# One end-of-block test with a whole-kernel repeat in place of four rechecks, and PSUM evacuations 300 places earlier in the order

## The chip, the cores and the metric

The kernel runs on one core of one Trainium2 chip. That core has five engines with queues of their own: TensorE (PE for matmuls, PEld for the load of the stationary operand), VectorE (DVE), ScalarE (ACT), GpSimd (POOL) and SyncE (SP), which issues nearly all DMAs. The metric is the device time of one execution in microseconds (us), lower is better.

## The reference

Two transformer blocks, one after the other, on one sequence of 1024 rows of width 1024, all in float32.

The first block has two layers. In each, the rows are normalised and modulated, projected, and go two ways: a spatial gating unit, and an attention in which every query row keeps only the 256 keys with the highest score of a small "indexer". That selection is what the change touches:

```python
logits = jnp.einsum('bthd,bsd->bths', qib, k_idx) * (IDX_DIM ** -0.5)
score = jnp.einsum('bth,bths->bts', wb, jax.nn.relu(logits)).astype(jnp.float32)
score = jnp.where(causal[None], score, -jnp.inf)
_, idx = lax.top_k(score, top)              # top = 256 of up to 1024 keys
...
p = jax.nn.softmax(sc, axis=-1).astype(v.dtype)
return jnp.einsum('bthk,btkd->bthd', p, v_sel)
```

The two ways are gated, concatenated, projected by `w_out`, added to the input and normalised. The second block (windowed attention, a short convolution, a router and 32 experts) follows; the change leaves its arithmetic alone.

## The kernel before

The program is written with a planner: Python code emits instructions in an order, each gets a priority from its place in that order, `tc.high_priority(offset=n)` places what it encloses n places further to the front, and the planner lays the instructions of every engine out on a simulated time line, taking the ready one with the best priority. On the chip each engine then runs its list strictly in that order.

A sequence is cut into 8 tiles of 128 rows, t or i = 0 to 7. Every float32 matmul is done with operands split in a high and a low part (`mm3`, L99 to L102: three matmuls); the split of a weight piece is an ACT copy (L108) and a POOL subtraction (L111).

One layer of the first block (`layer`) emits, in this order:

- for layer 2, the transposed input hT (`to_T`, L500: four PE transposes to one PSUM bank, then an ACT copy, L506, and a DVE subtraction, L507);
- projections (`dense_nat`), with `select` running beside them as two streams, tiles 2, 4, 6 and 3, 5, 7. `select(i)` transposes the indexer queries (`heads_T`, L535: PE L538, ACT L543, DVE L544), makes the scores (PE L628, ACT L631, DVE L634 and L636), scales them to 16-bit codes, stores the raw scores to DRAM (`scd`, L652), searches the threshold by counting (DVE L606 to L661), and takes the few remaining places by two MAX8. That handles at most 8 open places; a column of `fl` (L669) tells of a row with more. The result is a tile of 0 and -1e30, `bias[i]`, finished at L686;
- the gating unit `sgu`, a generator in the list `bgs` that is stepped beside the projections. It transposes its weights with `to_T` into `wmh` and `wml`, and its product leaves PSUM by one DVE instruction (L830);
- four pieces f = 0 to 3 of one more projection (`dense_T1`, PSUM banks `half`, evacuation L966 and L967), with the attention `attend` stepped beside them. It works in units of (tile, group, pair): `front` makes logits (PE L868), adds the bias and takes the row's extreme (DVE L869), exponentiates (ACT L872) and normalises (POOL L878); `back` transposes (PE L891), splits (ACT L899, DVE L900) and multiplies with the values (PE L904, L906); the pair of units ends with ACT L911 and DVE L912. Tiles 0 and 1 need only the causal bias; a tile from 2 on waits in `attend` until it is in `checked`;
- after piece f = 1 (`RA`) the emission of `select` is driven until tiles 4 and 5 are done, and then `recheck((2, 3, 4, 5))` is emitted; after 18 units (`RC`) `recheck((6, 7))`. A recheck adds the flags with a matmul (L752), reduces and compares them (DVE L754, L756), loads the answer into registers of DVE and SP (L757), takes three of the four buffers with the tag `w4` (the attention's `pt2` has the same tag), and opens a `tc.Switch` with two arms. Arm 1 loads the raw scores and computes the biases of these tiles exactly (`halves`, `choose`); arm 0 is empty. Since arm 1 writes `bias`, everything that reads `bias` of these tiles is behind the Switch;
- the load of `w_out` (L996, SP), split on ACT and POOL into the buffers `s32` that hT held, and the end of each tile: `fin1` (L1023, L1029, L1032) and `fin2` (48 matmuls on `half`, DVE L1045), with what is left of the attention.

At the very end of the program stands a loop `tc.For_i(0, nov, 1)` (L1735) over the experts' overflow blocks, whose count is loaded by every engine (L1730).

## Time and profile before

| | |
|---|---|
| time, median of 3 runs | 2373.92 us (2371.7 to 2374.93) |
| the profiled execution | 2371.94 us, span 2369.8 us |
| PE busy | 2140.5 us, 90% of the span |
| DVE busy | 1521.2 us, 64% |
| ACT and POOL busy | 1082.8 and 1082.0 us, 46% each |
| mean granted TensorE clock | 0.961 |

The span is the time from the first instruction to the last of that execution; the 2.1 us around it belong to the device time. Busy time counts an engine as working while an instruction runs; a matmul at the lower granted clock counts as busy for longer. Idle time in front of an instruction is put down to the semaphore that ended the wait. Layer 1 of the first block lies at about 45 to 690 us, layer 2 at 690 to 1320, the second block behind that.

### The profile page before, as it was taken

The numbers are of one execution on the slowest core, as the hardware profiler recorded it, in microseconds if no ns is written. First come the engines' busy times: TensorE is split into PE (matmuls) and PEld (weight loads), VectorE is DVE, ScalarE is ACT, GpSimd is POOL, SyncE is SP. The second block draws the span as 40 slices with busy tenths as digits, with TensorE's granted clock in tenths as the row PEclk, the third lists the DMA queues.
The fourth block names the chain that finished last, engine by engine and source line by source line (L and its number), as shares of the span: only waits on it lengthen the run. The fifth ranks groups of instructions, "written<-read, shape, count | busy, mean of one in ns | idle before, by whom it ended". The sixth has DMA issues, their size and how long they took to land. (4 is left out here: it accounts for less than half of the span.)

```text
span 2369.8 us, 35974 instructions
## 1 busy us (share of the span) xinstructions
PE 2140.5 (90%) x13235; PEld 1883.9 (79%) x13235; DVE 1521.2 (64%) x3191; ACT 1082.8 (46%) x1943; POOL 1082.0 (46%) x1018
## 2 busy tenths in 40 slices
PE   5998998798989979997998999999999797999896
PEld 4898897587879979876887888888888586888785
DVE  9768887677753769685776348861010345888784
ACT  4333443554642443436554335652121222778774
POOL 4664575556736553845554345532244412222221
PEclk9999998899999989998999999999999998999998
DMA  7522112312114111223111111122121256999994
GB/s 239 188 79 86 53 32 81 106 59 68 41 47 138 45 36 49 66 67 108 68 45 41 44 41 34 30 52 67 49 67 45 98 209 200 311 325 326 317 329 116
DMA packets 146392, 260.88 MB, mean 110 GB/s; under 512 B 24681, under 2 KB 101889, under 8 KB 133905
## 3 DMA queue, kind: packets, MB, share of 16 engines
q1 hardware_dynamic: 139024, 241.59, 31.1%
q0 software_dynamic: 7168, 16.79, 3.2%
q8 instruction: 105, 1.72, 0.3%
q14 instruction: 95, 0.77, 0.1%
HBM read 228.83 MB, written 37.90 MB: 113 GB/s over the span
## 5 line engine op out<-in xcount | busy, mean ns | idle before, releaser
L111 POOL TENSOR_TENSOR wlo<-wraw,whi 128x512 fp32r<-128x512 f32 (+1 forms) x188 | 249.8, 1329 | 484.9 <-ACT whi L108 459.2
L101 PE MATMUL big<-wlo,s 128*128 128x256 f32 (+1 forms) x1536 | 440.4, 288 | 16.0 <-POOL wlo L111 16.0
L100 PE MATMUL big<-whi,s 128*128 128x256 f32 (+1 forms) x1536 | 437.8, 289 | 13.6 <-ACT s L506 8.4
L102 PE MATMUL big<-whi,s 128*128 128x256 f32 (+1 forms) x1536 | 439.6, 288 | 0.0
L101 PEld LDWEIGHTS big<-wlo,s 128*128 128x128 f32 x1536 | 301.2, 196 | 22.8 <-POOL wlo L111 19.6
L100 PEld LDWEIGHTS big<-whi,s 128*128 128x128 f32 x1536 | 298.6, 196 | 21.9 <-ACT s L506 11.0
L102 PEld LDWEIGHTS big<-whi,s 128*128 128x128 f32 x1536 | 300.6, 196 | 3.1 <-issue 0.9
L108 ACT ACTIVATE whi<-wraw 128x512 fp32r<-128x512 f32 (+1 forms) x188 | 117.7, 627 | 385.2 <-PE big L102 127.2
L111 DVE TENSOR_TENSOR ew<-s,ew 128x1024 fp32r<-128x1024 f32 x138 | 162.8, 1220 | 39.0 <-ACT ew L108 37.9
L636 DVE SCALAR_TENSOR_TENSOR s<-rel,widx,s 128x384 f32<-128x384 f32 (+3 forms) x140 | 130.6, 957 | 85.1 <-ACT rel L631 83.6
L100 PE MATMUL sm<-ew,xT 128*96 128x256 f32 x512 | 147.6, 288 | 4.8 <-ACT xT L1636 4.8
L108 ACT ACTIVATE ew<-s 128x1024 fp32r<-128x1024 f32 x138 | 137.7, 1050 | 28.6 <-PE sm L102 18.8
L102 PE MATMUL sm<-ew,xT 128*96 128x256 f32 x512 | 148.6, 290 | 1.3 <-DVE xT L1637 1.2
L101 PE MATMUL sm<-ew,xT 128*96 128x256 f32 x512 | 146.3, 286 | 0.9 <-DVE ew L111 0.9
L631 ACT ACTIVATE rel<-sm 128x384 f32<-128x384 f32 (+3 forms) x160 | 80.5, 522 | 124.1 <-PE sm L628 114.7
L100 PE MATMUL half<-s,whi 128*128 128x512 f32 x320 | 130.7, 408 | 7.1 <-ACT s L953 3.1
L101 PE MATMUL half<-s,whi 128*128 128x512 f32 x320 | 128.7, 402 | 0.0
L102 PE MATMUL half<-s,wlo 128*128 128x512 f32 x320 | 127.3, 401 | 0.0
L1674 POOL DMA_INDIRECT out_dram<-yt,ti x32 | 58.2, 1820 | 136.0 <-DMA out_dram<-yt,ti 61.0
L606 DVE TENSOR_SCALAR_CACHE_REDUCE bias<-code,cand 128x512 bf16<-128x512 int16 (+5 forms) x126 | 114.1, 924 | 0.5
L878 POOL TENSOR_SCALAR Z<-Z,rc 128x128 f32<-128x128 f32 (+7 forms) x88 | 63.9, 738 | 83.3 <-DVE rc L876 50.7
L100 PE MATMUL big<-s,whi 128*128 128x512 f32 x256 | 99.7, 390 | 0.3 <-DVE convf L1335 0.3
(618 smaller groups left out, 6014.3 us busy)
## 6 DMA issues: line engine op xcount, KB each, us to landing
wraw<-in_w_in_dram SPq DMA_DIRECT2D x164, 256.0 KB, 2.8
adaw<-in_w_ada_dram SPq DMA_DIRECT2D x48, 512.0 KB, 4.5
s<-in_w_gate_e_dram SPq DMA_DIRECT2D x23, 1024.0 KB, 9.2
s<-in_w_up_e_dram SPq DMA_DIRECT2D x23, 1024.0 KB, 11.0
s<-in_w_down_e_dram SPq DMA_DIRECT2D x23, 1024.0 KB, 11.3
X<-in_w_gate_e_dram SPq DMA_DIRECT2D x9, 1024.0 KB, 10.1
X<-in_w_up_e_dram SPq DMA_DIRECT2D x9, 1024.0 KB, 9.8
X<-in_w_down_e_dram SPq DMA_DIRECT2D x9, 1024.0 KB
```

The source lines that it names most:

```text
L100: T.matmul(o, lh, rh, start=start, stop=False, skip_group_check=True)
L101: T.matmul(o, lh, rl, start=False, stop=False, skip_group_check=True)
L102: T.matmul(o, ll, rh, start=False, stop=stop, skip_group_check=True)
L108: A.activation(hi, src, AF.Copy)
L111: return (sub or V).tensor_tensor(lo, src, hi.bitcast(FT), op=OP.subtract)
L606: V.tensor_scalar(junk[:, :src.shape[1]], src, thr, 0.0, op0=op, op1=OP.add, accum_out=cnt)
L631: A.activation(rel[:, :w_], ps[:, :w_], AF.Relu, scale=0.125)
L636: V.scalar_tensor_tensor(d, rel[:, :w_], widx[:, i, h:h + 1], d, op0=OP.mult, op1=OP.add)
L878: G.tensor_scalar(P[hh][:, :n], P[hh][:, :n], rc[:, hh:hh + 1], 1.0, op0=OP.mult, op1=OP.mult)
L1674: return G.indirect_dma_start(out=out, out_offset=bass.IndirectOffsetOnAxis(ap=ycol, axis=0), in_=yt, in_offset=None, bounds_check=S - 1, ...
```

## The change

The four rechecks and the raw-score stores go. All twelve columns of flags are kept in one tile `fl`, added once after the second layer, and compared into `crowd`, a tile of one number that lives outside. The kernel's body becomes `tile_blocks`; the new `tile_hybrid` runs it, loads `crowd` into a register of every engine, and opens a loop of 0 or 1 turns around a second, complete copy of the body, in which `select` always takes the exact way. `attend` now lets a tile's units in as soon as that tile is in `bias`. Separately, the ACT and DVE instructions that empty the PSUM banks of `to_T`, of `heads_T` and of the gating unit get `tc.high_priority(offset=300)`; the transposes in front of them keep their places.

```diff
@@ -37,8 +37,20 @@
     return bass.AP(tensor=ap.tensor, offset=ap.offset, ap=[[0, 128], [1, n]])
 
 
+def tile_hybrid(tc, I, out):
+
+
+    nc = tc.nc
+    with ExitStack() as ctx:
+        crowd = ctx.enter_context(tc.tile_pool(name="crowd", bufs=1)).tile([1, 1], I32, name="crowd")
+        tile_blocks(tc, I, out, crowd)
+        more = nc.values_load(crowd[0:1, 0:1], min_val=0, max_val=1)
+        with tc.For_i(0, more, 1):
+            tile_blocks(tc, I, out)
+
+
 @with_exitstack
-def tile_hybrid(ctx, tc, I, out):
+def tile_blocks(ctx, tc, I, out, crowd=None):
     nc = tc.nc
     V, A, G, T = nc.vector, nc.scalar, nc.gpsimd, nc.tensor
 
@@ -165,6 +177,7 @@
     ZAB, ZBB, BGA, RC, RA = 2600.0, 1300.0, 3000.0, 18, 1
     due, now, dve = [0.0], [0.0], [0.0]
     ADC = 300.0
+    EV = 300
     HATT = 300
     FBK = 0, 1, 2, 3, 2
     HOLD, ZBK = 0, (0, 2, 3, 3)
@@ -503,8 +516,9 @@
             for j in range(4):
                 T.transpose(ps[:, j, :], src[:, (b * 4 + j) * 128:(b * 4 + j + 1) * 128], ident)
             d = (slice(None), slice(b * 4, b * 4 + 4), slice(t * 128, (t + 1) * 128))
-            A.activation(hi[d], ps, AF.Copy)
-            V.tensor_tensor(lo[d], ps, hi[d].bitcast(FT), op=OP.subtract)
+            with tc.high_priority(offset=EV):
+                A.activation(hi[d], ps, AF.Copy)
+                V.tensor_tensor(lo[d], ps, hi[d].bitcast(FT), op=OP.subtract)
 
     def rope(dst, src, t, H, eng):
 
@@ -540,8 +554,9 @@
         for g in range(2):
             q = pool.tile([128, 4, 128], FR, name=f"qT{g}", tag="qT", bufs=bufs)
             hi, lo = slice(64 * g, 64 * g + 64), slice(64 - 64 * g, 128 - 64 * g)
-            A.activation(q[hi], ps[hi], AF.Copy)
-            V.tensor_tensor(q[lo], ps[hi], q[hi].bitcast(FT), op=OP.subtract)
+            with tc.high_priority(offset=EV):
+                A.activation(q[hi], ps[hi], AF.Copy)
+                V.tensor_tensor(q[lo], ps[hi], q[hi].bitcast(FT), op=OP.subtract)
             r.append(q)
         return r
 
@@ -597,14 +612,16 @@
             dense_nat(256, 8, lhs, range(2, NT), ev_qi(c))
 
         bias, bias_ = {}, {}
-        fl = small1.tile([128, 6], BF, name="fl", bufs=1)
-        scd = dram.tile([128, 6, S], FT, name=f"scd{l}")
         headed, scored = set(), set()
 
         def count(src, thr, op, z, junk):
             cnt = small1.tile([128, 1], FT, name=f"cnt{z}")
             V.tensor_scalar(junk[:, :src.shape[1]], src, thr, 0.0, op0=op, op1=OP.add, accum_out=cnt)
             return cnt
+
+        def mask(sc, n):
+            G.affine_select(sc[:, n - 128:n], sc[:, n - 128:n], pattern=[[-1, 128]], compare_op=OP.is_ge,
+                            fill=-BIG, base=0, channel_multiplier=1)
 
         def select(i):
 
@@ -636,6 +653,16 @@
                             V.scalar_tensor_tensor(d, rel[:, :w_], widx[:, i, h:h + 1], d, op0=OP.mult, op1=OP.add)
                         yield 60.0 + 1.04 * w_, False, 0.0, 2 * w_ / 2.4
             scored.add(i)
+            if crowd is None:
+                mask(sc, n)
+                gt = bias_[i] = att.tile([128, n], BF, name=f"bias{i}")
+                up, lw, eq, pre = (tmp.tile([128, n], d, name=f"bits{j}", tag="r2", bufs=6)
+                                   for j, d in enumerate((I16, U16, BF, F16)))
+                c, cand = halves(i, sc, up, lw, gt)
+                choose(sc, gt, c, cand, 0, eq, pre)
+                yield 0.0, False, 0.0, 0.0
+                bias[i] = gt
+                return
 
 
 
@@ -646,10 +673,8 @@
             V.tensor_scalar(sq, ss, 1.0 / (n * 250.0 ** 2), 1e-15, op0=OP.mult, op1=OP.max)
             scl = small1.tile([128, 1], FT, name=f"few{z}", bufs=1)
             G.tensor_tensor(scl, sq, mhalf[:, :1], op=OP.pow)
-            G.affine_select(sc[:, n - 128:n], sc[:, n - 128:n], pattern=[[-1, 128]], compare_op=OP.is_ge,
-                            fill=-BIG, base=0, channel_multiplier=1)
+            mask(sc, n)
             A.activation(code, sc, AF.Identity, scale=scl[:, 0:1], bias=near[:, 0:1])
-            nc.sync.dma_start(scd[:, i - 2, :n], sc)
             gt = bias_[i] = att.tile([128, n], BF, name=f"bias{i}")
             yield 300.0, False, 2500.0 + n, 0.0
             cand = None
@@ -666,7 +691,7 @@
             cnt = count(code, cand[:, 0:1], OP.is_gt, z, gt)
             K2 = small1.tile([128, 1], FT, name=f"K2{z}", bufs=1)
             V.tensor_scalar(K2, cnt, -1.0, 256.0, op0=OP.mult, op1=OP.add)
-            V.tensor_scalar(fl[:, i - 2:i - 1], K2, 8.0, None, op0=OP.is_gt)
+            V.tensor_scalar(fl[:, 6 * l + i - 2:6 * l + i - 1], K2, 8.0, None, op0=OP.is_gt)
             V.scalar_tensor_tensor(sc, gt, -1e38, sc, op0=OP.mult, op1=OP.add)
             yield 400.0 + 1.3 * n, False, 0.0, 0.0
             m8 = small1.tile([128, 8], FT, name=f"m8{z}", bufs=1)
@@ -744,29 +769,6 @@
             V.tensor_tensor(eq, eq, pre, op=OP.mult)
             V.tensor_tensor(gt, gt, eq, op=OP.add)
             V.tensor_scalar(gt, gt, -1.0, BIG, op0=OP.add, op1=OP.mult)
-
-        def recheck(tiles):
-
-            a, b = tiles[0] - 2, tiles[-1] - 1
-            pf = bank([128, 512], "sm")
-            T.matmul(pf[0:1, a:b], ones, fl[:, a:b], start=True, stop=True)
-            f1 = small1.tile([1, 1], FT, name="f1", bufs=1)
-            V.tensor_reduce(f1, pf[0:1, a:b], axis=AX.X, op=OP.add)
-            fi = small1.tile([1, 1], I32, name="fi", bufs=1)
-            V.tensor_scalar(fi, f1, 0.5, None, op0=OP.is_ge)
-            many = nc.values_load(fi[0:1, 0:1], engines=(DVE, SP), min_val=0, max_val=1)
-            sct = tmp.tile([128, S], FT, name="sct", tag="w4", bufs=4)
-            wt = [tmp.tile([128, 2, S], I16, name="wt", tag="w4", bufs=4) for _ in range(2)]
-            for arm in tc.Switch({DVE: many, SP: many}, 2):
-                if arm == 1:
-                    for i in tiles:
-                        n = 128 * (i + 1)
-                        sc = sct[:, :n]
-                        up, lw = wt[0][:, 0, :n], wt[0][:, 1, :n].bitcast(U16)
-                        eq, pre = wt[1][:, 0, :n].bitcast(BF), wt[1][:, 1, :n].bitcast(F16)
-                        nc.sync.dma_start(sc, scd[:, i - 2, :n])
-                        c, cand = halves(i, sc, up, lw, bias_[i])
-                        choose(sc, bias_[i], c, cand, 0, eq, pre)
 
         def stream(tiles):
             for i in tiles:
@@ -827,7 +829,8 @@
                 ps = bank([128, NT, 64], "sm")
                 mm3(ps, wmh[:, g, :], wml[:, g, :], vs[:, 0], vs[:, 1], True, True)
                 xu = X[:, :, 1, g * 64:(g + 1) * 64]
-                V.scalar_tensor_tensor(xu, ps, bs[:, g:g + 1], xu, op0=OP.add, op1=OP.mult)
+                with tc.high_priority(offset=EV):
+                    V.scalar_tensor_tensor(xu, ps, bs[:, g:g + 1], xu, op0=OP.add, op1=OP.mult)
                 yield SG3, 660.0
 
         bgs.append(sgu())
@@ -912,7 +915,7 @@
                 V.tensor_tensor(yg, pov[0:64], yg, op=OP.add)
             free.extend(taken.pop(u))
 
-        done, fronts, checked = [0], [0], {0, 1}
+        done, fronts = [0], [0]
 
         def attend():
             while done[0] < len(units):
@@ -920,7 +923,7 @@
                 while fronts[0] < len(units):
                     f = fronts[0]
                     t = units[f][0]
-                    if f > u + 3 or len(free) < (1 if t < 4 else 2) or t not in checked:
+                    if f > u + 3 or len(free) < (1 if t < 4 else 2) or t > 1 and t not in bias:
                         break
                     front(f)
                     fronts[0] += 1
@@ -976,8 +979,6 @@
             dense_T1(8, lambda k, a: hT[a][:, k, :], ev_zb(f), ZBB)
             if f == RA:
                 bg_until(lambda: {4, 5} <= set(bias))
-                recheck((2, 3, 4, 5))
-                checked.update((2, 3, 4, 5))
         bgs.clear()
         while done[0] % 2:
             next(att_)
@@ -1068,9 +1069,6 @@
                 if next(att_, None) is None:
                     break
             bg(BGA)
-            if done[0] >= RC and 6 not in checked:
-                recheck((6, 7))
-                checked.update((6, 7))
             if done[0] == seen:
                 continue
             seen = done[0]
@@ -1089,6 +1087,7 @@
         bank_plan(2, 0, 2, 2)
         return xout
 
+    fl = small1.tile([128, 12], BF, name="fl", bufs=1)
     ones = const.tile([128, 1], BF, name="ones")
     V.memset(ones, 1.0)
     onesf = const.tile([128, 1], FT, name="onesf")
@@ -1115,6 +1114,12 @@
     rope_tables(first_h(hT0))
     x1 = layer(0, x0, hT0)
     x2 = layer(1, x1)
+    if crowd is not None:
+        pf = bank([128, 512], "sm")
+        T.matmul(pf[0:1, 0:12], ones, fl, start=True, stop=True)
+        f1 = small1.tile([1, 1], FT, name="f1", bufs=1)
+        V.tensor_reduce(f1, pf[0:1, 0:12], axis=AX.X, op=OP.add)
+        V.tensor_scalar(crowd, f1, 0.5, None, op0=OP.is_ge)
     b1.close()
```

## Rows read from the trace of the kernel before

**Rows 1.** The page's first part: the span, then each engine's busy time with its share of the span.

```profile
span 2369.8 us, 35974 instructions
PE 2140.5 (90%) x13235; PEld 1883.9 (79%) x13235; DVE 1521.2 (64%) x3191; ACT 1082.8 (46%) x1943; POOL 1082.0 (46%) x1018
```

**Rows 2.** The table by stretches: start and end, length, then busy us and instructions of PE, PEld, DVE, ACT and POOL, the granted clock, the DMA share and GB/s.

```profile
440.00:480.00 40.00, 23.84 (x102) 18.53 (x102) 20.36 (x53) 25.09 (x59) 26.60 (x28) 0.70 0.40 126
480.00:690.00 210.00, 193.29 (x1114) 162.77 (x1113) 156.00 (x371) 113.77 (x200) 132.33 (x98) 0.99 0.16 52
...
830.00:880.00 50.00, 37.02 (x251) 35.22 (x250) 35.66 (x73) 19.66 (x40) 27.96 (x21) 0.83 0.13 37
...
1060.00:1100.00 40.00, 27.21 (x125) 21.66 (x123) 17.05 (x48) 24.42 (x56) 24.14 (x27) 0.74 0.42 127
```

**Rows 3.** The same table, two stretches of 20 us of layer 1.

```profile
400.00:420.00 20.00, 19.08 (x91) 15.79 (x91) 19.84 (x52) 7.68 (x20) 3.98 (x6) 0.96 0.21 67
...
500.00:520.00 20.00, 19.80 (x121) 17.40 (x120) 15.64 (x45) 11.88 (x23) 12.56 (x11) 1.00 0.11 41
```

**Rows 4.** The time line of DVE in layer 1: the instructions that finish the biases of tile 2 (384 columns; that of tile 3 was finished before it) and of tile 4 (640 columns; that of tile 5 before it).

```profile
211.21 0.25 DVE L686 TENSOR_SCALAR bias<-bias 128x384 bf16<-128x384 bf16 x1
...
325.43 0.86 DVE L686 TENSOR_SCALAR bias<-bias 128x640 bf16<-128x640 bf16 x1
```

**Rows 5.** The time line of DVE around the first recheck of layer 1, and then around that of layer 2 (start, us, instruction; in brackets the idle time before it and what ended it): the last reading of a row extreme of tile 1, and the first row extreme of tile 2.

```profile
444.99 0.08 DVE L869 DVE_READ_ACCUMULATOR2_ANT mx<- 128x1 f32 x1
...
454.51 0.56 DVE L869 CUSTOM_DVE_ANT_0 Z<-sm,bias 128x384 f32<-128x384 f32 x1
...
1072.47 0.09 DVE L869 DVE_READ_ACCUMULATOR2_ANT mx<- 128x1 f32 x1
...
1083.24 0.56 DVE L869 CUSTOM_DVE_ANT_0 Z<-sm,bias 128x384 f32<-128x384 f32 x1 [0.47 <-issue]
```

**Rows 6.** The time line of ACT and then that of PE behind the first recheck of layer 1.

```profile
450.46 0.63 ACT L108 ACTIVATE s<-wraw 128x512 fp32r<-128x512 f32 x1 [4.03 <-DMA wraw<-in_w_out_dram]
...
447.01 1.06 PE L538 MATMUL tr<-ident,X 128*128 128x128 f32 x4
...
452.40 1.01 PE L868 MATMUL sm<-kst,qT 128*128 128x384 f32 x2 [3.69 <-DVE qT L544]
```

**Rows 7.** The time line of DVE where tile 2 of layer 1 gives way to tile 3, with no recheck between them.

```profile
469.19 0.08 DVE L869 DVE_READ_ACCUMULATOR2_ANT mx<- 128x1 f32 x1
...
475.01 0.69 DVE L869 CUSTOM_DVE_ANT_0 Z<-sm,bias 128x512 f32<-128x512 f32 x1 [0.17 <-PE sm L868]
```

**Rows 8.** Groups by line within 440 to 480 us (count, busy us, mean ns, idle before it and what ended that), and the first matmul of `fin2` in the time line of PE.

```profile
L111 POOL TENSOR_TENSOR s<-wraw,s 128x512 fp32r<-128x512 f32 x16 | 20.6, 1304 | 10.0 <-ACT s L108 8.5 <-DMA wraw<-in_w_out_dram 1.4
...
480.31 0.50 PE L100 MATMUL half<-s,yah 128*128 128x512 f32 x1
```

**Rows 9.** The time lines of DVE, ACT and PE around the transposed weights of the gating unit in layer 2.

```profile
840.66 0.69 DVE L507 TENSOR_TENSOR wml<-tr,wmh 128x512 fp32r<-128x512 f32 x1
...
841.41 2.26 PE L538 MATMUL tr<-ident,Z 128*128 128x128 f32 x8 [8.97 <-DVE wml L507]
...
832.42 1.08 ACT L506 ACTIVATE wmh<-tr 128x512 fp32r<-128x512 f32 x2
```

**Rows 10.** Waits of PE over the whole span: who waited for whom, us in total, times, longest.

```profile
PE big L101 <- POOL wlo L111: 16.0, 8, 5.1
...
PE big L100 <- ACT s L506: 8.4, 7, 5.4
...
PE sm L868 <- DVE qT L544: 7.7, 2, 4.0
...
PE smx L868 <- DVE qT L544: 4.1, 2, 2.8
```

**Rows 11.** From the views of L506 and of L543: how long ACT sat idle before L506 until PE's transposes were done (us, times); the instructions of L543 on the bank `tr`, and the same idle time before L543.

```profile
  PE tr L504: 26.3, 19
...
L543 ACT ACTIVATE qT<-tr x46: 573/592/596, 127.5 to 1405.4; 64x512 fp32r<-64x512 f32 x46
...
  PE tr L538: 17.3, 7
```

**Rows 12.** The view of the raw-score stores, the wait of SP's own queue for a recheck's answer, and the view of L752: the flag matmuls of the two second rechecks.

```profile
L652 SPq DMA_DIRECT2D scd<-s x12: 325/338/353, 159.5 to 1000.5; - x12
...
SPq L757 <- DVE fi L756: 14.9, 2, 14.6
...
L752 PE MATMUL sm<-fl,ones x2: 164/164/164, 510.8 to 1137.6; 128*1 128x2 bf16 x2
```

**Rows 13.** The loop at the end, by the views of L1730, L1735 and L1774 (the last is put on waits and branches that have no line of their own): instruction, count, ns least/median/most, first and last start.

```profile
L1730 POOLq EVENT_SEMAPHORE  x5: 17/43/43, 2357.3 to 2357.6; - x5
L1735 PEldq EVENT_SEMAPHORE  x14: 51/51/51, 2351.8 to 2363.8; - x14
L1735 PEldq COMPARE_BRANCH  x3: 96/163/322, 2350.5 to 2363.9; - x3
L1735 POOLq COMPARE_BRANCH  x3: 33/41/50, 2358.4 to 2363.6; - x3
L1735 POOLq INC_SWDGE_SEM  x1: 1464/1464/1464, 2358.6 to 2358.6; - x1
L1774 POOLq DRAIN  x3: 46/98/5302, 2363.7 to 2369.6; - x3
```

## The prediction

> **What bounds the kernel now.** I read the page's busy shares first, then the table by stretches, then, in the stretches where TensorE does least, the time lines. PE is busy for 90% of the span and no other engine for more than 64% [rows 1], so the kernel is bound by PE's work nearly everywhere, and a change gains only where PE stands or runs at its lower clock. Three stretches of the first block stand out [rows 2]. From 440 to 480 us PE is busy for 23.84 of 40 us at a mean granted clock of 0.70, which is 23.84 x 0.70 = 16.7 us of full-speed work: 23.3 us are lost. From 1060 to 1100 it is 27.21 x 0.74 = 20.1, so 19.9 are lost. From 830 to 880 it is 37.02 x 0.83 = 30.7 of 50, so 19.3 are lost. The first two are the same place in the two layers, the first recheck; the third is the gating unit of layer 2. Behind 480 us PE is busy for 193.29 of 210 us at 0.99 [rows 2], so work that is drawn forward into one of these holes shortens the layer.
>
> **The recheck in the holes.** The biases of tiles 2 and 4 are ready at 211.5 and 326.3 us [rows 4], but no bias is read before 454.51 [rows 5]: everything that reads one stands behind the Switch, and the Switch wants three of the four `w4` buffers, which the attention of tiles 0 and 1 holds. That attention is slow for another reason: DVE is busy for 19.84 of 20 us [rows 3], by the order of the streams with the search for tiles 6 and 7. Its last row extreme is read at 445.07, and the first one of tile 2 begins at 454.51: 9.4 us; in layer 2 it is 1083.24 - 1072.56 = 10.7 [rows 5]. Between tiles 2 and 3, with no recheck between them, the same step takes 475.01 - 469.27 = 5.7 us [rows 7]. So the recheck costs the attention's chain at least 3.7 + 5.0 us. More of it goes by the evacuation: after the Switch the transposed queries are complete on PE at 448.1, but ACT, whose order has a split of `w_out` first, stands for 4.03 us for that DMA, and PE goes on at 452.40 [rows 6]. With the evacuation 300 places earlier I take 4 us for the step instead of 5.7, so 9.4 - 4 = 5.4 and 10.7 - 4 = 6.7: 12.1 us gained. The hole doesn't close: `fin2` can only start at 480.31, when `w_out` is split, and its 16 pieces of 1.30 us on POOL follow the death of hT [rows 8]. So there are bounds. If `w_out` alone set the end of the hole, only PE's own share of the stretch, 16.7 / 40 = 42% of 12.1, would count: 5 us. If half of both losses came back, 21.6. I take 12.1, nearer to the rows of the chain, because the stalled splits of ACT stand in that same wait.
>
> **The evacuations.** In layer 2 ACT has emptied the gating unit's weights into `wmh` at 833.5, but DVE gets to `wml` only at 840.66, behind the end of a search; the bank is held, and PE, which wants it for transposes, stands 8.97 us [rows 9]. Placed ahead, the two subtractions of 0.69 us run about 7 us earlier. Not all of it stays: DVE is busy with the same work either way, and the logits behind those transposes wait for it. But PE comes back at the lower clock, a mean of 0.83 over this stretch [rows 2], and that part is saved. I take 6.5; bounds 0 (the logits stand instead) and 12 (the 9.0 and half of the stretch's clock loss, 0.17 x 37 / 2 = 3). The other evacuations are seldom queued: at hT PE waited 8.4 us for ACT, at the queries 7.7 and 4.1 for DVE, of which 3.69 and the longest, 4.0, are counted above [rows 6, 10]; ACT itself stood for the transposes for 26.3 us at hT and 17.3 at the queries, so mostly it is PE that is late and an earlier place gives nothing [rows 11]. I take 2, bounds 0 and 5. In the second block's attention and behind it I take 0.
>
> **What costs nothing.** The twelve stores of raw scores are 12 x 0.34 = 4.1 us of SP's queue [rows 12], hidden, since SP mostly waits for free buffers; bounds 0 and -1. SP's wait for a recheck's answer, 14.6 us at most [rows 12], belongs to a second recheck; that of layer 1 is at 510.8 [rows 12], and PE is busy for 19.80 of 20 us there [rows 3], so 0, and up to -2. The one matmul and two DVE instructions of the new test stand between the blocks, 0.2 us if not hidden.
>
> **What is added.** After the overflow loop every engine loads `crowd`, compares, and jumps over a second program. Nothing but the end is queued behind that wait, but the end is the path. No row shows a jump over so much; the nearest is the overflow loop, which takes no turn here. On POOL its test begins at 2357.3 and the branch is at 2358.4: 1.1 us. Then come a semaphore step of 1.46, 14 waits of at most 0.05 us, 0.7, and two more branches of up to 0.16, 0.3 [rows 13]. That is about 3.6 us again. PE, which jumps furthest, needs 1.3 us more, from its branch at 2350.5 to its next wait at 2351.8, where POOL goes on after 0.2 [rows 13]. The Trainium skill (Runtime: NRT & Kernel Launch, Instruction fetch mechanics) says that a taken branch whose target isn't in the two pages held must wait for a fetch; PE's 1.3 us agree, and it speaks against this change, since all five engines now jump over a second program of 35974 instructions [rows 1]. I take 3.6 and two thirds of PE's 1.3, since only the last engine to arrive sets the end: 4.5. Below: 0, if POOL's last drain of 5.30 us [rows 13] only counts from the last scatter and hides it. Above: the whole of 2357.3 to 2363.6 once more and PE's jump, 7.6.
>
> **The sum.** -12.1 - 6.5 - 2 + 4.5 = -16.1. From the profiled execution's 2371.94 that is 2355.8; the median of the three runs lies 1.98 higher, so 2357.8 us.
>
> **The rivals.** *The holes fill.* Attention of tile 2 may slip between the matmuls of the dense pieces, and `w_out` start earlier: 21.6 back, 9 at the gating unit, 5 at the others, 2.5 at the end: -33, about 2341. For it: biases ready 130 to 240 us before use [rows 4, 5]. Against: DVE is full there [rows 3], and the attention's probabilities have two buffers until then.
> *The hole stays.* `w_out` sets its end: -5, -1 where the logits stand, 0 elsewhere, and 5.4 at the end: about 2373. For it: POOL's 20.6 of 40 us and 10.0 waiting [rows 8].
> *Slower, by the evacuations.* ACT's order is strict. An evacuation that the planner puts ahead of a weight split, with transposes that come later on the chip than planned, holds the split, POOL's subtraction behind it, and then PE. Before the change 7 evacuations of the queries stood 17.3 us, 2.5 each [rows 11], and PE waited 16.0 us for split weights [rows 10]. If all 46 on bank `tr` stood 2.5 us, ACT would stand 115 us. If a fifth of that reaches PE, 23 us, the result is -16.1 + 23 = +6.9, about 2381; it decides from 16.1 + 4.7 = 20.8 us on.
> *It doesn't do what it says.* If a flag were set, the body would run twice, above 4700 us. Between 445.07 and 454.51 [rows 5] there is no room for the 4 x 31 counts of a recheck's second arm, so these inputs set none.
>
> **How the numbers follow.** Chances: forecast 0.50 (2347 to 2368), holes fill 0.18, hole stays 0.17, slower 0.14, repeat 0.01. A difference under 0.2%, 4.7 us, can't be told from none here. Half of "hole stays" lies within that, a quarter on either side; so faster 0.50 + 0.18 + 0.04 = 0.72, same 0.09, slower 0.14 + 0.01 + 0.04 = 0.19. The range goes from 2336, past the filled holes, to 2375, past the hole that stays; it leaves out the slow rival and a little below.
>
> **What would show it.** Right: no L752 to L757 between the layers; the first read of a bias within 5 us of the last row extreme of tile 1; PE over 28 of 40 us in the stretches of the rechecks; no 9 us wait at `wml`; 4 to 5 us more between the last scatter and the end. Wrong: `fin2` starting as late as now after the last dense piece; PE's waits for split weights far above 16 us; an end longer by over 8 us; a loss in a stretch that the change doesn't touch, by the planner's new order.

## The result and the profile after

The changed kernel takes 2392.72 us (median of 4 runs, 2391.09 to 2393.66) against 2372.81 us before on the same chip (2368.84 to 2374.93): ratio 1.0082, 95% interval 1.0064 to 1.01. It is 19.9 us slower. Forecast were 2357.8 us and faster.

The page of the changed kernel starts as below. Its mean granted clock is 0.964, before it was 0.961. TensorE has the same work: the columns that its matmuls stream (512 for one with an output of 128x512), added up from the trace, are 4183652 in both kernels. It is busy for 16 us more, and the rest of the 19.6 us of span is idle time [rows 1].

```profile
span 2389.4 us, 35894 instructions
PE 2156.5 (90%) x13232; PEld 1880.1 (79%) x13232; DVE 1510.4 (63%) x3185; ACT 1085.4 (45%) x1943; POOL 1085.2 (45%) x1018
```

The table by stretches (columns as in [rows 2]): first the kernel before in the 40 us behind each hole, then the changed kernel in the holes and behind them.

```profile
480.00:520.00 40.00, 39.80 (x235) 34.37 (x235) 30.80 (x81) 23.57 (x48) 18.89 (x19) 1.00 0.16 54
1100.00:1140.00 40.00, 39.66 (x234) 34.17 (x235) 31.55 (x82) 25.18 (x54) 18.97 (x19) 1.00 0.16 54
```

```profile
440.00:480.00 40.00, 29.33 (x158) 20.87 (x156) 27.57 (x77) 25.97 (x63) 12.20 (x19) 0.96 0.31 104
480.00:520.00 40.00, 32.43 (x156) 23.89 (x157) 18.65 (x48) 22.03 (x41) 28.66 (x26) 0.96 0.30 93
1060.00:1100.00 40.00, 34.91 (x175) 27.38 (x173) 20.35 (x56) 19.98 (x49) 9.94 (x16) 0.93 0.14 46
1100.00:1140.00 40.00, 31.08 (x131) 22.05 (x132) 18.99 (x48) 22.34 (x47) 23.57 (x23) 0.80 0.45 145
```

The hole at 440 us did fill: 29.33 x 0.96 = 28.2 us of full-speed work where 16.7 were done [rows 2]. That product says too much, though. Over the whole span it is 22 us larger than before (2156.5 x 0.964 against 2140.5 x 0.961) for exactly the same matmuls. Counted in columns, the stretch has 38912 where it had 25860, half as much again, and the next 40 us have 55104 where they had 78722. So a new hole stands right behind the old one, and together the two stretches do less than before. POOL shows whose the new hole is. It is busy for 12.20 of 40 us where it had 26.60 [rows 2], and for 28.66 in the next 40. The time line of DVE says the same of the attention: from the last row extreme of tile 1 to the first of tile 2 the step is now 445.49 - 445.01 = 0.5 us in layer 1 and as much in layer 2, where it took 9.4 and 10.7 [rows 5].

```profile
444.93 0.08 DVE L872 DVE_READ_ACCUMULATOR2_ANT mx<- 128x1 f32 x1
445.49 0.56 DVE L872 CUSTOM_DVE_ANT_0 Z<-smx,bias 128x384 f32<-128x384 f32 x1 [0.48 <-PE smx L871]
...
1081.64 0.08 DVE L872 DVE_READ_ACCUMULATOR2_ANT mx<- 128x1 f32 x1
1082.20 0.56 DVE L872 CUSTOM_DVE_ANT_0 Z<-smx,bias 128x384 f32<-128x384 f32 x1 [0.48 <-PE smx L871]
```

What became late is `w_out`. First SP's own queue in the kernel before (L996 loads `w_out`, the first two pieces at 424.43; L279 loads a modulation row), then in the changed kernel (L997 and L292; L1026 loads the residual rows `rt`); the second number is the time from the first to the last of a merged row.

```profile
424.43 2.81 SPq L996 DMA_DIRECT2D wraw<-in_w_out_dram  x2
...
447.10 20.69 SPq L996 DMA_DIRECT2D wraw<-in_w_out_dram  x12
475.53 0.33 SPq L279 DMA_DIRECT2D scale<-modd  x1
```

```profile
463.76 0.32 SPq L292 DMA_DIRECT2D scale<-modd  x1
464.13 5.76 SPq L1026 DMA_DIRECT2D rt<-in_x_dram  x3
469.94 10.34 SPq L997 DMA_DIRECT2D wraw<-in_w_out_dram  x5
...
482.55 16.58 SPq L997 DMA_DIRECT2D wraw<-in_w_out_dram  x10
```

Before, the loads of `w_out` came first and `scale1` and `rt` behind them. Now they come last, and SP stands in front of `scale1`. The time line of POOL before, then those of POOL, ACT and PE in the changed kernel: POOL's first split of `w_out` comes 36 us later, right behind the attention's `pth` (L902), while `fin2` starts at 479.95, as early as before [rows 8], and then runs into weights that are not there.

```profile
440.24 4.17 POOL L111 TENSOR_TENSOR s<-wraw,s 128x512 fp32r<-128x512 f32 x3 [4.51 <-ACT s L108]
```

```profile
475.90 1.28 POOL L123 TENSOR_TENSOR s<-wraw,s 128x512 fp32r<-128x512 f32 x1 [2.88 <-ACT s L120]
...
472.36 0.58 ACT L902 ACTIVATE pth<-tr 128x512 fp32r<-128x512 f32 x1
...
479.95 0.50 PE L112 MATMUL half<-s,yah 128*128 128x512 f32 x1
```

The waits of SP's queue and of PE in that stretch (who waited for whom, us in total, times, longest):

```profile
SPq L292 <- DVE pt L903: 18.6, 1, 18.6
...
PE half L113 <- POOL s L123: 6.4, 9, 2.3
```

The product with the gate behind `fin2` tells what stays of it. From the view of that line in each layer (L1045 before, L1046 after; first and last start): in layer 1 it begins 4 us and ends 7 us later, in layer 2 it begins 21 and ends 16.5 us later. From there to the last scatter the changed kernel takes 1052.3 us and the kernel before 1056.3. In that part, which the change hardly touches, the profiles of this section and the next range from 1049 to 1060 us, so the 4 us are within what single executions differ by.

```profile
L1045 DVE TENSOR_TENSOR s<-half,gate x16: 671/690/693, 488.7 to 677.1; 128x512 f32<-128x512 f32 x16
...
L1045 DVE TENSOR_TENSOR s<-half,gate x16: 673/688/693, 1114.5 to 1301.2; 128x512 f32<-128x512 f32 x16
```

```profile
L1046 DVE TENSOR_TENSOR s<-half,gate x16: 673/692/693, 492.8 to 684.5; 128x512 f32<-128x512 f32 x16
...
L1046 DVE TENSOR_TENSOR s<-half,gate x16: 681/692/693, 1135.2 to 1317.7; 128x512 f32<-128x512 f32 x16
```

The gating unit's place looks as it did. DVE in the kernel before, then DVE and PE in the changed one: the subtraction into `wml`, now at 845.99, still stands behind the same 1.75 us of the search, and PE still waits for it, 7.72 us where it was 8.97 [rows 9].

```profile
838.88 1.75 DVE L683 SCALAR_TENSOR_TENSOR bias<-s,lcand,bias 128x512 bf16<-128x512 f32 x1
```

```profile
844.21 1.75 DVE L708 SCALAR_TENSOR_TENSOR bias<-s,lcand,bias 128x512 bf16<-128x512 f32 x1
...
846.74 2.26 PE L552 MATMUL tr<-ident,Z 128*128 128x128 f32 x8 [7.72 <-DVE wml L521]
```

The end, from the views of the loop's lines (L47 loads `crowd`, L48 tests and jumps, L1779 is the end; columns as in [rows 13]; the rows of POOL's branches and waits are those from 2378.5 us on), then the last scatter, and that of the kernel before. From the scatter to POOL's first drain it is 2383.2 - 2370.0 = 13.2 us; before it was 2363.7 [rows 13] - 2357.53 = 6.2. So the end is 7.0 us longer.

```profile
L47 POOLq TENSOR_LOAD <-crowd x1: 304/304/304, 2376.3 to 2376.3; - x1
...
L48 POOLq EVENT_SEMAPHORE  x12: 42/43/43, 2382.1 to 2383.0; - x12
L48 POOLq COMPARE_BRANCH  x2: 33/36/38, 2378.8 to 2383.1; - x2
...
L48 PEldq COMPARE_BRANCH  x3: 70/184/3743, 2377.2 to 2382.8; - x3
L48 POOLq INC_SWDGE_SEM  x1: 1435/1435/1435, 2377.3 to 2377.3; - x1
...
L1779 POOLq DRAIN  x3: 46/98/5302, 2383.2 to 2389.1; - x3
...
2370.04 1.41 POOL L1679 DMA_INDIRECT out_dram<-yt,ti  x1 [4.68 <-DMA out_dram<-yt,ti]
```

```profile
2357.53 1.41 POOL L1674 DMA_INDIRECT out_dram<-yt,ti  x1 [5.00 <-DMA out_dram<-yt,ti]
```

### The profile page after: what moved, and what is told of

It is laid out like the page before. It is cut to its first block, busy times and chain, and to the rows that moved or that the text cites. A ratio compares the mean times of both kernels' runs of the same rounds, so it can differ in the third digit from the quotient of the medians.

```text
span 2389.4 us, 35894 instructions
## 1 busy us (share of the span) xinstructions
PE 2156.5 (90%) x13232; PEld 1880.1 (79%) x13232; DVE 1510.4 (63%) x3185; ACT 1085.4 (45%) x1943; POOL 1085.2 (45%) x1018
## 3 DMA queue, kind: packets, MB, share of 16 engines
q8 instruction: 107, 1.75, 0.3%
## 5 line engine op out<-in xcount | busy, mean ns | idle before, releaser
L112 PEld LDWEIGHTS big<-whi,s 128*128 128x128 f32 x1536 | 295.2, 194 | 20.0 <-ACT s L520 9.1
L114 PEld LDWEIGHTS big<-whi,s 128*128 128x128 f32 x1536 | 297.3, 194 | 3.8 <-issue 0.9
L881 POOL TENSOR_SCALAR Z<-Z,rc 128x128 f32<-128x128 f32 (+7 forms) x96 | 69.1, 733 | 131.3 <-DVE rc L879 97.3
L875 ACT ACTIVATE Z<-Z,mx 128x128 f32<-128x128 f32 (+7 forms) x96 | 67.3, 701 | 79.2 <-DVE mx L872 78.4
```

The costliest lines, as they stand in the source:

```text
L112: T.matmul(o, lh, rh, start=start, stop=False, skip_group_check=True)
L114: T.matmul(o, ll, rh, start=False, stop=stop, skip_group_check=True)
L875: e = A.activation(Pv, Pv, AF.Exp, bias=mx[:, npart - 1:npart], scale=-1.0, accum_out=sm[:, hh:hh + 1])
L881: G.tensor_scalar(P[hh][:, :n], P[hh][:, :n], rc[:, hh:hh + 1], 1.0, op0=OP.mult, op1=OP.mult)
```

## The experiments

Each median stands beside that of the kernel before, run on the same chip; those lie between 2372.8 and 2374.2 us. The chips differ from one group of runs to the next. Behind a ratio stands its 95% interval. The first four part the change and try the first theory: SP's order holds `w_out` back.

**e1: the flags alone.**

```
-    EV = 300
+    EV = 0
```

> The changed kernel with its evacuations back in their old places (offset 0 instead of 300): the flags' part and the loop alone. Theory Q (queue): without the Switch, SP's queue has the loads of scale1 and rt, which wait for w4 buffers that the attention holds, ahead of the loads of w_out; w_out is split 20 us later, and this has nothing to do with the evacuations. Then this kernel loses what the changed one loses, and the little that the evacuations gave: 2391 to 2399 us, the first load of w_out again behind the loads of rt. Rival E (evacuations): the early places stall ACT and DVE; then without them the loss of 17 us in the layers is gone and about 2376 us is left (before and 7 us of the end).

2388.38 us, ratio 1.0054 (1.0029 to 1.0079). 14.2 of the 19.9 us of loss are here without any evacuation moved, so rival E, which gave 2376, falls; the first load of `w_out` is at 473.0 us. Whether the other 5.7 us are the evacuations' is open, as the intervals overlap.

**e2: the evacuations alone.** The kernel before, with the three places of the diff of the change (`to_T`, `heads_T`, the gating unit's product) and nothing else of it:

```
+    EV = 300
...
+            with tc.high_priority(offset=EV):
+                A.activation(hi[d], ps, AF.Copy)
+                V.tensor_tensor(lo[d], ps, hi[d].bitcast(FT), op=OP.subtract)
```

> The kernel before with the evacuations of to_T, heads_T and the gating unit 300 places earlier; rechecks and Switches as before, no loop. Theory Q: 2365 to 2373 us, that is no loss, since w_out's loads stay ahead of rt on SP; my recorded terms for the evacuations, 6.5 and 2 us, would give 2364. Rival E: 2380 to 2392 us.

2372.79 us, ratio 0.9998 (0.9977 to 1.0018). Neither a loss nor the forecast gain.

**e3: no loop at the end.**

```
-        more = nc.values_load(crowd[0:1, 0:1], min_val=0, max_val=1)
-        with tc.For_i(0, more, 1):
-            tile_blocks(tc, I, out)
```

> The changed kernel without the loop at the end: the sum of the flags is computed but not loaded, and the body is in the program once. From the traces the last scatter's begin to POOL's last drain took 13.2 us in the changed kernel and 6.2 before, so 7.0 us should come back: 2385.7 us. Rival: the second copy of the program costs elsewhere too (code loading during the run); then more than 10 us come back, below 2382. If it costs less than its row says because the drain hides it, 2390 or more.

2383.37 us, ratio 1.0041 (1.0028 to 1.0054): 9.4 us less than the changed kernel by the medians, where its rows say 7.0. The intervals don't tell the two apart, so a second cost is not shown. In the profiles of all kernels, the stretch from the last scatter to POOL's first drain takes 12.6 to 13.2 us in the nine that have the loop and 6.1 to 6.4 in the six that don't.

**e4: `w_out` first on SP.** L999 loads `w_out` here. `wod` lists these loads in order, and `follow` makes one instruction wait for another. By the code, `rt` waits for the twelfth load, and `scale1` for the last, not for the twelfth as the expectation has it.

```
-            mod_row(scale1, 1, 1)
...
+            follow(nc.sync.dma_start(scale1, rows_of(modd[4], D)), wod[-1], "behind w_out")
...
             d = nc.sync.dma_start(rt, xin[t * 128:(t + 1) * 128, :])
+            follow(d, wod[11], "behind w_out")
```

> The changed kernel with one order on SP's queue undone: the load of scale1 and the loads of rt wait for loads of w_out (scale1 and rt follow the twelfth), so w_out's loads stand ahead of them again. Theory Q: w_out is split from 441 us on instead of 475, fin2 of layer 1 starts some 12 to 17 us earlier, and the same in layer 2: 2358 to 2372 us. Rival A (attention ahead of the dense pieces: hT is freed late, or DVE and ACT are full with the attention, so w_out can't be used earlier): 2388 to 2394, or a gain under 5 us. Rival E: the same, no gain.

2394.81 us, ratio 1.0092 (1.0068 to 1.0116): no gain. My theory fell, and the trace says why. SP's queue, then its waits, then POOL's first split:

```profile
446.17 36.16 SPq L999 DMA_DIRECT2D wraw<-in_w_out_dram  x5
...
504.82 0.33 SPq L1069 DMA_DIRECT2D scale<-modd  x1
...
SPq L999 <- DVE ptl L903: 29.6, 1, 29.6
...
477.01 1.29 POOL L123 TENSOR_TENSOR s<-wraw,s 128x512 fp32r<-128x512 f32 x1 [1.76 <-ACT s L120]
```

The first load goes out at 446.17, and the second stands 29.6 us for `ptl`, the attention's lower half. So `w_out` waits for a buffer that the attention holds. Even the piece that was loaded at once is split only at 477.01: ACT's order, laid out by the planner, has its copy (at 476.30) behind the copies into `pth`. In `back`, a unit's probabilities go into `pth` with the tag `wraw` as soon as `done[0] >= SD and not bgs`, and these are the three buffers through which `w_out` is loaded. Before, the planner has written out 12 units when it comes to those loads; with the gate open at once the count is 13 after the dense pieces, the `while done[0] % 2` makes it 14, and unit 13 lands in `wraw` ahead of `w_out`. The traces bear the count out: ACT copies into `pt`, the buffer used otherwise, 16 times a layer before and 18 times in the changed kernel, which is 12 units and 13 (one copy for a unit of tiles 0 and 1, two for one of tiles 2 and 3).

**e5: unit 13 out of the staging buffers.** One constant tests this.

```
-    SD, WOE = 12, 17
+    SD, WOE = 14, 17
```

> The changed kernel with SD = 14 instead of 12: the attention's unit 13 (tile 3), which is now written out before the loads of w_out, keeps its probabilities in a w4 buffer instead of two of the three wraw buffers through which w_out is loaded. Theory W (staging): the gate's early opening makes the planner write out 14 units ahead of w_out instead of 12, unit 13's probabilities stand in w_out's staging buffers, and that alone makes w_out wait for the attention of tiles 2 and 3. Then its splits run from about 441 us again, the 17 us lost in the two layers come back, 2376 us, and with the holes of my prediction filled by half 2364: 2358 to 2378. Rival A (the attention fills ACT, DVE and POOL first, and w_out is late whatever its buffers are): 2388 to 2394.

2374.31 us, ratio 1.0011 (0.9996 to 1.0026): 18.4 us come back by the medians, 17 by the ratios. SP's queue and the stretches of this kernel:

```profile
443.34 21.46 SPq L997 DMA_DIRECT2D wraw<-in_w_out_dram  x11
470.62 0.33 SPq L292 DMA_DIRECT2D scale<-modd  x1
```

```profile
440.00:480.00 40.00, 28.25 (x135) 20.40 (x136) 25.57 (x65) 29.35 (x67) 27.82 (x31) 0.86 0.38 121
600.00:640.00 40.00, 34.93 (x182) 28.94 (x181) 29.85 (x66) 20.21 (x33) 30.99 (x21) 0.91 0.13 47
```

`w_out` stands ahead of `scale1` again, with nothing done to SP's order: that order was a consequence of the buffers. The hole is filled in part (28.25 x 0.86 = 24.3 us of work for 16.7; in columns 32256 for 25860, a quarter more). But from 600 to 640 us PE does 34.93 x 0.91 = 31.8 us, and in the kernel before 37.4; in columns 62016 and 68736, so what was gained in the hole is given back there, and layer 1 ends where it did (last gate product at 676.6, before at 677.1).

```profile
600.00:640.00 40.00, 37.36 (x220) 30.93 (x219) 32.60 (x82) 25.97 (x45) 33.66 (x24) 1.00 0.14 47
```

**e6: the old gate, no recheck.** A set `gated` in the planner, emptied where the rechecks stood.

```
-                    if f > u + 3 or len(free) < (1 if t < 4 else 2) or t > 1 and t not in bias:
+                    if f > u + 3 or len(free) < (1 if t < 4 else 2) or t in gated:
...
+                gated -= {2, 3, 4, 5}
...
+            if done[0] >= RC:
+                gated.clear()
```

> The changed kernel, still without rechecks and Switches, but with the old gate in the planner: no unit of tiles 2 to 5 before the second dense piece, none of tiles 6 and 7 before unit 18, so that 12 units are written out ahead of w_out, as before. Theory W: w_out is early again and the recheck's own cost is gone: 2392.7 - 17 - (0 to 12) = 2364 to 2376 us. Rival A: no unit is drawn forward past the old gate, so it gives up to 17 us as well, but then e5_sd14 gives nothing. Rival S (the Switch itself kept SP and DVE in a good order): 2388 to 2394.

2385.17 us, ratio 1.0047 (1.0022 to 1.0071), 9 us above the range. `w_out` is early (its splits start at 443.6 us), so it is 7.5 us faster than the changed kernel, but the hole is still there, and so is the step from tile 1 to tile 2:

```profile
440.00:480.00 40.00, 25.20 (x117) 19.86 (x115) 18.77 (x50) 26.41 (x60) 27.27 (x28) 0.74 0.43 138
...
446.78 0.08 DVE L872 DVE_READ_ACCUMULATOR2_ANT mx<- 128x1 f32 x1
455.02 0.56 DVE L872 CUSTOM_DVE_ANT_0 Z<-smx,bias 128x384 f32<-128x384 f32 x1
```

That is 25.20 x 0.74 = 18.6 us of work, hardly more than 16.7, and a step of 455.02 - 446.86 = 8.2 us, where the kernel with the recheck has 9.4 [rows 5]. Taking the Switch out fills nothing as long as the planner opens the gate late; it is the earlier opening that fills the hole.

**e7: SD = 14, evacuations in their old places.** The kernel of e5 with the edit of e1.

```
-    EV = 300
+    EV = 0
...
-    SD, WOE = 12, 17
+    SD, WOE = 14, 17
```

> SD = 14 as in e5_sd14, with the evacuations in their old places (offset 0). The two part by what the early places are worth where w_out is no longer late: my recorded terms say 8.5 us (this one slower by so much than e5_sd14); the run of the evacuations alone gave 0 to 4 us either way, by which the two are the same within 4 us.

2370.99 us, ratio 0.9986 (0.997 to 1.0001): 3.3 us below e5 by the medians, with intervals that overlap.

**e8: the fault without the change.** In the kernel before:

```
-        while done[0] % 2:
+        while done[0] < 14:
```

> The kernel before, with its rechecks, gate and old evacuations, and with one edit: the planner writes out 14 units of the attention ahead of the loads of w_out instead of 12. Units 12 and 13 then keep their probabilities in wraw, the staging buffers of w_out, as unit 13 does in the changed kernel. Theory W (staging): w_out is late here too, and the loss of the changed kernel's layers appears without any of its change: 10 to 25 us, 2384 to 2398 us. Rival A (it is the attention's freedom, not the buffers; here the old gate and the Switch are still there): 2368 to 2380.

2399.58 us, ratio 1.0103 (1.0077 to 1.0129): 26.8 us slower, and SP's queue looks as in the changed kernel.

```profile
473.52 0.34 SPq L279 DMA_DIRECT2D scale<-modd  x1
...
483.22 8.08 SPq L996 DMA_DIRECT2D wraw<-in_w_out_dram  x6
```

**e9: the same with SD = 14.**

```
-    SD, WOE = 12, 17
+    SD, WOE = 14, 17
```

> As e8_before_14ahead, 14 units ahead of the loads, but with SD = 14, so that units 12 and 13 use w4 buffers and wraw is w_out's alone. Theory W: the loss of e8 is gone, 2368 to 2380 us. If it is the two more units ahead of the loads that cost (PE, ACT and DVE being busy with them), not the buffers, it stays within 4 us of e8.

2389.98 us, ratio 1.0066 (1.0044 to 1.0088). The buffers give back 9.6 of the 26.8 us, and 17.2 stay although `w_out` is early here (its splits run from 440.6 to 473.2 us). Both expectations missed. With the old gate, two more units ahead of the loads cost by themselves. The trace shows where: `fin2` starts 8.8 us later than before in layer 1 (480.31 before [rows 8]), and 23.4 us later in layer 2 (1129.78 against 1106.41; 5 of them come from layer 1), with its weights ready.

```profile
489.13 0.48 PE L100 MATMUL half<-s,yah 128*128 128x512 f32 x1
```

Units 12 and 13, which the old gate keeps behind the recheck, now stand ahead of `fin2` in the planner's order. That this is the reason was not tested.

**e10: what the rechecks' removal is worth.** The kernel of e7 without the loop at the end (the three lines taken out for e3).

> The kernel of e7_sd14_ev0 (SD = 14, old places of the evacuations) without the loop at the end; the sum of the flags is computed and not used. What is left of the change is the removal of the rechecks and their Switches and the attention's earlier start. By e7 (2371.0) and the 7 us of the end's rows: 2364 us. My recorded term for the rechecks, -12.1, would give 2361.5; if the filled hole is given back later in the layer, as the windows of e5_sd14 show (7.6 us more work from 440 to 480 us, 5.5 less from 600 to 640), 2366 to 2372.

2364.66 us, ratio 0.9966 (0.9952 to 0.9979): 8.2 us below the kernel before. Against e7, which ran on another chip, the loop costs 2370.99 - 2364.66 = 6.3 us by the medians and 4.7 by the ratios.

**e11: SD = 16, evacuations in their old places.** The kernel of e7 with one constant more:

```
-    SD, WOE = 14, 17
+    SD, WOE = 16, 17
```

> The changed kernel with SD = 16 and the old places of the evacuations: all of the attention's tile 3 keeps its probabilities in w4. Theory W needs only unit 13 out of wraw, so this is within 4 us of e7_sd14_ev0, 2367 to 2375 us; more pressure on w4 (rt and scale1 wait for it) would make it slower, up to 2380.

2368.09 us, ratio 0.9982 (0.9961 to 1.0004), within what was expected. The next two runs repeat it (e13) beside its twin with the early evacuations (e12).

> SD = 16 with the evacuations 300 places earlier, in five rounds. By e5_sd14 against e7_sd14_ev0 (1.0011 and 0.9986) the early places cost about 3 us where w_out is not late; then 2370 to 2374 us, slower than e13_sd16_ev0 by 1 to 5 us. If that difference was chance, both are the same within 1.5 us. My recorded terms, a gain of 8.5 us, would give 2360.

> The kernel of e11_sd16_ev0 in five rounds, beside e12_sd16_ev300 on one chip: SD = 16, evacuations in their old places, rechecks gone, the loop at the end kept. From e11: 2366 to 2371 us, 0.1 to 0.3% below the kernel before.

2372.78 us, ratio 0.9995 (0.9979 to 1.0011), for e12, and 2369.88 us, ratio 0.9988 (0.9971 to 1.0004), for e13. The early places look 2.9 us dearer by the medians; the intervals overlap, so a cost is not shown, and a gain of 8.5 us is excluded. With the loop kept, SD = 16 has the lowest medians. That it is faster than SD = 14, or than the kernel before, is not shown.

## Why the prediction was wrong

By the medians of the runs the 19.9 us can be parted along a chain of kernels: -8.2 for rechecks and gate, with SD = 14 (e10 against before), +6.3 for the loop (e7 against e10), +3.3 for the evacuations (e5 against e7, not resolved from nothing), and +18.4 for `w_out` behind unit 13 (the changed kernel against e5). That they add up is no proof, since each step starts where the last one ends, and the kernels ran on different chips: by their intervals the single parts are uncertain by some 3 to 6 us. Forecast were -12.1, +4.5, -8.5 and nothing. The profiles bear out the largest part: the last gate product of layer 2 starts at 1316.7 to 1320.6 us in the four kernels with unit 13 in front of `w_out` (the changed one, e1, e3, e4), at 1291.7 to 1300.2 in the six with SD = 14 or 16 and the early gate, and at 1301.2 and 1304.2 in the kernel before and in e2.

**The step that failed** is in the part on the holes: "`fin2` can only start at 480.31, when `w_out` is split, and its 16 pieces of 1.30 us on POOL follow the death of hT". I took the start of that load as fixed by hT, which it was before: the last dense matmul ends at 439.2, and ACT's first copy for the split starts at 439.54. So `w_out` being late stands in my sum with nothing, and it measured 18.4 of the 36.0 us between the forecast change of -16.1 and the measured 19.9; another 11.8 are the evacuations, 3.9 the rechecks, 1.8 the loop. The forecast's last "wrong" sign, a loss by the planner's new order, names the family, but I put no price on it. The edit of the gate is also an edit of how far the planner gets before it comes to `w_out`. Once it is one unit farther, a rule in a line that the diff doesn't touch, `done[0] >= SD`, hands two of the three staging buffers to the attention. The rows of before show nothing of this, for the condition was met only behind the loads there; the code did show it. e5 takes the cause away, and e8 brings it into the kernel before without the change, though e9 shows that e8's loss has a second part.

**The recheck in the holes** was right that the wait would go, and wrong on whose it was and on its size. The step between the tiles fell to 0.5 us instead of 4, shorter by 8.9 and 10.2 us. Tile 2 starts 9.0 us earlier in layer 1 and, since layer 1 ended 7 us later, 1.0 us earlier in layer 2. Of the 19 us only 8.2 arrive at the end, less than the 12.1 that I took and above the lower bound of 5. The row from 600 to 640 us of e5 is one place where PE gives back what the hole gained; which wait sets the end of a layer then was not tried. e6 corrects the reason: without the recheck but with the old gate the step is still 8.2 us, so the hole belonged to the late opening of the gate, not to the recheck's work.

**The evacuations**, -6.5 and -2, failed. I took the offset of 300 places for an earlier place in time. At `wml` DVE keeps its order, with the same instruction ahead of it, and runs at the same point of the search; PE's wait changed by 1.25 us. e2's time line shows the same neighbour. My reading is that an offset moves an instruction only as far as the planner's own times let it; that was not tested. What the evacuations would be worth there, had they moved, wasn't tried.

**The loop at the end** was right in kind, and 4.5 was too small: 6.3 by the runs, 7.0 by the rows, within the bounds of 0 to 7.6. POOL needs 6.9 us from loading `crowd` at 2376.3 to its drain at 2383.2, so nothing of it is hidden. Test and semaphore step held: priced at 1.1 + 1.46, they take until 2378.8, which is 2.5. The waits nearly did: priced at 0.7, they run from 2382.1 to 2383.0. The term that was mis-sized is the jump. I gave it 0.9, two thirds of 1.3 us that I read as PE's jump in the overflow loop, and let POOL itself go on after 0.2. Those 1.3 us show no jump: PE was still at a matmul, which ends at 2351.79, and the next wait starts there.

```profile
2351.39 0.40 PE L102 MATMUL big<-ew,hdT 128*96 128x512 f32 x1
```

In the changed kernel POOL's branch is at 2378.8 and its next step at 2382.1, 3.2 us behind, on its own queue. PE's branch took 3.74 us, but it ran beside POOL's step and jump. The Trainium skill (Runtime: NRT & Kernel Launch, Instruction fetch mechanics) states that a taken branch to a target outside the pages held must wait for a fetch; this trace agrees, with 3.74 us where PE's longest branch in the overflow loop took 0.32 [rows 13].

**The rivals.** "Slower, by the evacuations" came nearest in time, 2381, but by luck: e2 shows no loss by its mechanism, and e1 has most of the loss without it. "The hole stays" was right that `w_out` would set the hole's end, and wrong that it would start no later than before. The body ran once: no second pass is in the trace. The signs named for "right" were met for the bias and for PE's 28 of 40 us in both holes, 29.33 and 34.91, and the result was still the other way. The sign at `wml` was not met, and the end missed its 4 to 5 us by 2. Of the signs for "wrong", `fin2` started as late as before and ran into weights that were not split: 6.4 us of waits from 430 to 520 us, nearly all of the 7 us by which layer 1 ends later.

**What was put at nothing**, the stores, the second rechecks and the new test, is inside e10's 8.2 us; no run parts it from the rest.

## What to carry to other kernels

When a change lets a planner write work out earlier, look at every rule that depends on how far it has got (a buffer chosen by a counter, a tag shared between stages), not only at the waits that go. A tag shared by the attention and a weight load makes the order in which the buffers are asked for a dependency, and putting the load first on SP's queue did not get past it; one constant was worth 17 to 18 us. When a theory about a queue's order seems plain, change that order alone first, as e4 did: nothing came back, and the waits of SP named the buffer. Busy time multiplied by the granted clock is no measure of work (here it was 22 us larger for the same matmuls); compare the matmuls themselves when the question is how much work a stretch did.

## What the hardware showed that I had not expected

A loop that takes no turn still costs 6 to 7 us when its body is the whole program. All engines must jump over it, and each pays for itself: from its branch to its next step it takes 2.4 us on ACT, 2.9 on SP and DVE, 3.2 on POOL and 3.7 on PE. ACT is through all its steps at 2380.2, before PE's branch ends at 2381.4, so they aren't waiting for one another there. The queues that the profile calls "instruction" are at work in that time (queue, packets, MB, share; from 2376 to 2384 us), and in the kernel before they move nothing from 2358 to 2364 us, its end.

```profile
q14 instruction: 8, 0.07, 2.6%
q8 instruction: 2, 0.03, 2.0%
```

ACT, DVE and PE reach the end at 2380.4, 2381.6 and 2383.0 us, and POOL, at 2383.2, last; only then does its drain of 5.30 us begin, which before started at 2363.7 [rows 13], so the drain hid none of it.
